# More places for the memory's raw weights and for blocks of x, and an order for down's first operands, in a hybrid decoder block

## The chip, the cores and the metric

One core of a Trainium2 chip runs the whole block in one launch. The time is device microseconds of one execution; the times below are whole executions, the trace is one profiled execution of the kernel, and its rows count from the start of its span.

## The reference

One layer over x (1024 rows of 1024, float32): forgetting attention and stick-breaking attention side by side, cross-attention onto 256 memory rows, and a gated feed-forward part with a short causal convolution. Cut to what matters:

```
h = rmsnorm(x); fq, fk, fv, sq, sk, sv, f_logit = split(h @ w_in)
fox = softmax(fq fk' / 8 + c_t - c_s) fv            # 8 heads of 64, c = cumsum(log_sigmoid(f_logit + b))
sb[t, s] = sigmoid(z) * prod_{s<j<t}(1 - sigmoid(z[t, j]));  sb_o = sb sv     # z = sq sk' / 8
x = x + concat(rmsnorm(fox), rmsnorm(sb_o)) @ w_out
k, v = split(rmsnorm(mem) @ w_mkv)                  # memory: 4 heads of 256
x = x + softmax(rmsnorm(x) w_mq k' / 16) v @ w_mo
u = causal_dwconv(rmsnorm(x) @ w_up, width 3);  gate, val = split(u)
x = x + (silu(gate) * val) @ w_down                 # w_down: 2816 -> 1024
out = rmsnorm(x)
```

## The kernel before

Every product is made of three matmuls of rounded operands: a value is split into a high half (rounded, by ACT or POOL) and a low half (the rest, by DVE), and hi x hi, lo x hi and hi x lo are added up in PSUM (lines 208 to 210). So each weight costs a load into a raw buffer, a high half ("whi") and a low half ("wlo"), each in two parts of 512 columns (lines 402, 407, 412), before PE can use it. The same lines serve all weights of this stage, which are numbered in the order of their use.

**The planned stage.** From line 355 on, the attention with the projections that run beside it is not written in program order: a planner ("Plan") takes operations with an engine, a cost, a due time and counted places, and makes one order for each engine's in-order queue. Score groups pass through "st" (scores, PE), exponentials (ACT), "aw" (a running sum, DVE), a multiply (POOL, line 703), transposes "pt" (PE), their split "pth" (ACT) and "ptl" (DVE), and the product "po" (PE). Between them PE makes projections: at the end of the stage those of the memory ("pk" for keys, "pmv" for values, evacuated to "mk" and "mv"), whose weights are 24 to 39, and then the first mixed products ("pm", the output projection w_out, weights from 40 on). The raw weights stand in a ring of three buffers of 512 columns ("wraw").

**Slots.** Four places of 4096 columns (slots 0 to 3) are used one after another for different things. Slot 3 is free once the last scores of the stick-breaking heads have been read (the key `qkdone["s", 3, 1, 1, "read"]`). It then takes "mxf0", the first half of the mixed rows, written earlier to memory by the stores of the heads' outputs and loaded again by 8 loads (line 865); those are the moving operand of the first pm products.

**Blocks of x.** The output of the first mixed products goes onto x, block by block (8 blocks of 256 rows by 512 columns): a load (line 876), adds by DVE (line 893), a store (line 880). The blocks use a ring of two places, tag "negc". Later the rows of x are loaded again ("xr", line 1025) for the second half of the mixed product. The last row of attention weights has a place of its own, tag "p7", which is free after the last transposes (`chain[0]`).

**Down.** After the up products the down product runs as Strassen-like products over 11 blocks f of the 2816 rows, ordered by the tile framework's own scheduler. Its first product takes the left half of a (the gated values, stored to memory as "a_d") and of w_down: for each f a load of a and of the weight (lines 1847, 1848), then a split of each ("opa", "opb", lines 1537 and 1540). Lines 1856 and 1857 load what later products want of the weights (the right halves and "B22"), line 1920 and POOL's accumulating loads what they want of a. All of them but POOL's are issued by SyncE's queue (SP).

## Time and profile before

| what | us |
|---|---|
| whole executions, median of 3 | 1589.77 (1586.8 to 1596.92) |
| profiled execution | 1587.33 |
| its span | 1585.5 |
| PE busy | 1523.2 |
| DVE busy | 1206.8 |
| ACT busy | 789.8 |
| POOL busy | 534.9 |
| mean granted clock of PE | 0.992 |

The span is what the trace shows, from the first instruction to the last; 1.83 us of the profiled execution lie around it. PE is busy nearly throughout, so a reader looks for the few places where PE is idle or where its matmuls take longer (the granted clock below 1.00), and goes from there to the instruction that released it, and to what that one had waited for.

### The profile page before, as it was taken

To read this page: it belongs to the slowest core of one execution; us is meant where nothing else is said; L and a number is where in the kernel's file an instruction comes from. 1 tells how busy PE (TensorE), PEld (TensorE's weight loads), DVE (VectorE), ACT (ScalarE), POOL (GpSimd) and SP (SyncE) were. 2 spreads that over 40 slices of the span, in tenths; PEclk is the share of its full clock that TensorE was granted. 3 is DMA by queue.
4 is the path that set the end of the run, shared out by engine and by line. 5 is a ranking of instruction groups with operands and counts; after the bars stand their busy time and mean duration, and the time that the engine had idled before them with its cause. 6 is when DMAs were issued, how large, how long until landed. Compare 5 with 4: busy or idle time off the path is not lost.

```text
span 1585.5 us, 22098 instructions
## 1 busy us (share of the span) xinstructions
PE 1523.2 (96%) x7684; PEld 1267.5 (80%) x7684; DVE 1206.8 (76%) x2066; ACT 789.8 (50%) x1558; POOL 534.9 (34%) x656
## 2 busy tenths in 40 slices
PE   7999999999999889999999989999999999999997
PEld 7677888887888767878887767888888888788886
DVE  7377877877877875364548899999999999786575
ACT  7368768767867652043325564333333333445445
POOL 3032323332331310123132256544455442233342
PEclk9999999999999999999999999999999999999999
DMA  5221021011025547412136554222222223998782
GB/s 180 88 74 67 20 69 61 28 67 67 28 67 167 200 146 248 153 50 77 40 107 174 127 164 126 81 93 88 85 80 80 80 82 106 326 293 203 147 185 106
DMA packets 78223, 183.54 MB, mean 116 GB/s; under 512 B 8728, under 2 KB 8856, under 8 KB 77856
## 3 DMA queue, kind: packets, MB, share of 16 engines
q1 hardware_dynamic: 62976, 152.63, 28.1%
q0 software_dynamic: 14688, 29.37, 10.4%
q8 instruction: 60, 0.98, 0.3%
q14 instruction: 51, 0.42, 0.1%
q10 hardware_dynamic: 448, 0.14, 0.0%
HBM read 130.69 MB, written 33.59 MB: 104 GB/s over the span
## 4 chain that ended last, share of the span: by engine, by line
PE 57%; DVE 19%; issue 8%; ACT 7%; DMA 6%; POOL 2%; SPq 0%; POOLq 0%; DVEq 0%; ACTq 0%
PE dn L209 4%; PE dn L210 4%; PE dn L208 4%; PE pt L746 3%; PE up_p L208 3%; PE up_p L209 3%; PE up_p L210 3%; PE pq L208 2%; PE pq L209 2%; PE pq L210 2%; PE po L763 2%; PE pqm L210 2%; DMA wraw<-in_w_dram 2%; PE pqm L209 2%; PE pqm L208 2%
## 5 line engine op out<-in xcount | busy, mean ns | idle before, releaser
L703 POOL TENSOR_TENSOR p<-p,aw 128x383 f32<-128x383 f32 (+4 forms) x64 | 79.6, 1243 | 173.5 <-DVE aw L697 148.9
L750 ACT ACTIVATE pth<-pt 128x512 fp32r<-128x512 f32 x192 | 92.7, 490 | 61.1 <-PE pt L746 55.2
L754 DVE TENSOR_TENSOR ptl<-pt,pth 128x512 fp32r<-128x512 f32 x192 | 103.6, 549 | 25.5 <-ACT pth L750 24.0
L209 PE MATMUL dn<-opb,opa 128*128 128x512 f32 x308 | 120.7, 392 | 2.3 <-DVE opb L1540 2.3
L210 PE MATMUL dn<-opb,opa 128*128 128x512 f32 x308 | 120.6, 391 | 0.0
L208 PE MATMUL dn<-opb,opa 128*128 128x512 f32 x308 | 118.9, 391 | 0.0
L746 PE MATMUL pt<-zid,p 128*128 128x128 f32 x576 | 95.7, 275 | 4.7 <-DVE ptl L754 4.5
L746 PEld LDWEIGHTS pt<-zid,p 128*128 128x128 f32 x576 | 72.6, 142 | 23.9 <-DVE ptl L754 6.9
L1551 POOL TENSOR_TENSOR tmp<-wv 128x512 f32<-128x512 f32 x20 | 33.5, 1674 | 164.1 <-DMA wv<-in_w_dram 158.5
L412 DVE TENSOR_TENSOR wlo<-wraw,whi 128x512 fp32r<-128x512 f32 x84 | 68.0, 838 | 21.5 <-ACT whi L407 21.0
L763 PE MATMUL po<-ptl,v 128*128 128x512 f32 x192 | 68.6, 357 | 9.0 <-DVE ptl L754 8.7
L1779 ACT ACTIVATE yv<-cv,cw 128x1024 f32<-128x1024 f32 x22 | 27.3, 1242 | 99.7 <-DVE cv L1811 98.4
L194 POOL TENSOR_SCALAR whi<-wraw 128x512 fp32r<-128x512 f32 x48 | 30.0, 639 | 134.4 <-issue 44.6
L680 POOL TENSOR_SCALAR p<-p,fx 128x128 f32<-128x128 f32 (+3 forms) x64 | 48.7, 764 | 74.6 <-DVE fx L620 63.9
L209 PEld LDWEIGHTS dn<-opb,opa 128*128 128x128 f32 x308 | 58.1, 189 | 14.6 <-DVE opb L1540 2.7
L208 PE MATMUL up_p<-b,a 128*128 128x512 f32 x176 | 69.3, 394 | 0.0
L762 PE MATMUL po<-pth,v 128*128 128x512 f32 x192 | 68.5, 357 | 0.5 <-ACT pth L750 0.4
L210 PE MATMUL up_p<-b,a 128*128 128x512 f32 x176 | 68.5, 389 | 0.0
L209 PE MATMUL up_p<-b,a 128*128 128x512 f32 x176 | 68.5, 389 | 0.0
L208 PEld LDWEIGHTS dn<-opb,opa 128*128 128x128 f32 x308 | 58.3, 189 | 12.3
L210 PEld LDWEIGHTS dn<-opb,opa 128*128 128x128 f32 x308 | 58.3, 189 | 12.2
L407 ACT ACTIVATE whi<-wraw 128x512 fp32r<-128x512 f32 x84 | 49.9, 626 | 30.6 <-DMA wraw<-in_w_dram 14.8
(513 smaller groups left out, 5227.8 us busy)
## 6 DMA issues: line engine op xcount, KB each, us to landing
wraw<-in_w_dram SPq DMA_DIRECT2D x136, 256.0 KB, 3.0
a_d<-yv SPq DMA_DIRECT2D x22, 512.0 KB, 2.6
wg<-in_w_dram SPq DMA_DIRECT2D x20, 512.0 KB, 3.5
wv<-in_w_dram SPq DMA_DIRECT2D x20, 512.0 KB, 3.5
dn<-a_d POOLq DMA_DIRECT2D x32, 256.0 KB, 7.0
dn<-a_d SPq DMA_DIRECT2D x24, 256.0 KB, 9.2
dn<-in_w_dram SPq DMA_DIRECT2D x24, 256.0 KB, 7.9
xr<-mos POOLq DMA_DIRECT2D x20, 256.0 KB, 6.1
```

Of the source, the lines that this page charges most:

```text
L208: T.matmul(o, lt[0], rt[0], start=start, stop=False)
L209: T.matmul(o, lt[0], rt[1], start=False, stop=False)
L210: T.matmul(o, lt[1], rt[0], start=False, stop=stop)
L407: A.activation(t["hi"][:, c], t["raw", n], AF.Copy)
L412: in_turn("low", lambda: V.tensor_tensor(t["lo"][:, c], t["raw", n], t["hi"][:, c].bitcast(F32), op=ALU.subtract))
L680: G.tensor_scalar(out=c_["p"], in0=c_["p"], scalar1=c_["fx"][:, 4:5], scalar2=0.0, op0=ALU.mult, op1=ALU.add)
L703: G.tensor_tensor(c_["p"][:, :n0 - 1], c_["p"][:, :n0 - 1], c_["a"][:, 1:], op=ALU.mult)
L746: T.transpose(pt[:, j * P:(j + 1) * P], self.rows[j]["p"][:, kb * P:(kb + 1) * P], ident)
L750: A.activation(t[:, 512 - n:], self.sp["pt", kb][:, 512 - n:], AF.Copy)
L754: V.tensor_tensor(t[:, 512 - n:], self.sp["pt", kb][:, 512 - n:], self.sp["th", kb][:, 512 - n:].bitcast(F32), op=ALU.subtract)
L762: T.matmul(self.po[:, c], lv, self.sp["th", kb][:, c], start=kb == 0, stop=False)
L763: T.matmul(self.po[:, c], lv, self.sp["tl", kb][:, c], start=False, stop=kb == 4 * self.g + 3)
```

## The change

- Weights 26 to 37 no longer use the ring of three buffers. Their raw halves go to eight buffers "rx", views of slot 3, which are made when the last stick-breaking scores have been read. The loads of mxf0 into the same slot wait for the last low half that reads rx (`rx_end`). The planner orders the stage anew with these places.
- The sixth and the eighth block of x (those with t2 == 3) use the place of p7, after the last transposes; the others stay in the ring of two.
- In down, the splits of the first product are tied in order (f = 0, 1, 2 ...; each behind the last high half and low half before it). The loads of the second set wait for the issue of the first sixteen loads of the first set, and the loads of a's right halves with POOL's additions for that of the 22 second loads.

```diff
@@ plan
+    RX, rx, rx_end = range(26, 38), [], []
+        raw = "rx" if i in RX else "raw"
             def load(n=n, c=c):
-                t["raw", n] = wp.tile([P, 512], F32, tag="wraw", name=f"wraw{i}", bufs=3)
+                if raw == "rx":
+                    t["raw", n] = rx[(2 * i + n) % 8]
+                else:
+                    t["raw", n] = wp.tile([P, 512], F32, tag="wraw", name=f"wraw{i}", bufs=3)
-            l_ = plan.add(DMA, 900, load, [], ["raw"], at=at, late=1800, behind=b_[0][0])
+            l_ = plan.add(DMA, 900, load, [], [raw], at=at, late=1800, behind=b_[0][0])
-            o_ = plan.add(DVE, dve(512), low, [h_], ["lo"] * (n == 0), ["raw"], at=at, lock=True, behind=b_[0][2])
+            o_ = plan.add(DVE, dve(512), low, [h_], ["lo"] * (n == 0), [raw], at=at, lock=True, behind=b_[0][2])
+            if raw == "rx":
+                rx_end[:] = [o_]
...
-        for th, k, after in ((0, 3, [qkdone["s", 3, 1, 1, "read"]]), (1, 0, line[-1:])):
+        for th, k, after in ((0, 3, rx_end), (1, 0, line[-1:])):
...
+            t = pp.tile([P, D], F32, tag="p7", name="xs") if late_x(nh, t2) else \
+                sw.tile([P, D], F32, tag="negc", name="xs", bufs=2)
...
-                        x_[nh, tb // 2] = plan.add(DMA, 900, lambda nh=nh, tb=tb: load_x(nh, tb // 2), [], ["negc"],
+                        x_[nh, tb // 2] = plan.add(DMA, 900, lambda nh=nh, tb=tb: load_x(nh, tb // 2), chain[0] * late_x(nh, tb // 2),
+                                                   [place(nh, tb // 2)],
...
+            plan.add(DMA, 0, lambda: rx.extend(views(slot(3, "rx", dt=F32).rearrange("p k c -> p (k c)"), 8)), [qkdone["s", 3, 1, 1, "read"]], [], ["rx"] * 8, at=0)
@@ down
-    for f in range(H):
-        nc.sync.dma_start(pb[f][:, hi_], w[dn0 + f, :, hi_])
-        nc.sync.dma_start(B22[f], w[dn0 + H + f, :, hi_])
+    with ExitStack() as behind:
+        for l_ in first_loads[:2 * 8]:
+            behind.enter_context(tc.issue_after(l_.ins))
+        for f in range(H):
+            second_loads += [nc.sync.dma_start(pb[f][:, hi_], w[dn0 + f, :, hi_]),
+                             nc.sync.dma_start(B22[f], w[dn0 + H + f, :, hi_])]
...
-            split_op(oa, fa(f), A)
-            split_op(ob, fb(f), A)
+            for dst, src in ((oa, fa), (ob, fb)):
+                with ExitStack() as behind:
+                    for ins in queue:
+                        behind.enter_context(tc.issue_after(ins))
+                    low = split_op(dst, src(f), A)
+                if in_order:
+                    queue[:] = last_round[0], low
...
-    o = dn_product(lambda f: pa[f][:, lo_], lambda f: pb[f][:, lo_])
+    o = dn_product(lambda f: pa[f][:, lo_], lambda f: pb[f][:, lo_], in_order=True)
...
+    with ExitStack() as behind:
+        for l_ in second_loads[:22]:
+            behind.enter_context(tc.issue_after(l_.ins))
+        for f in range(H):
+            nc.sync.dma_start(pa[f][:, hi_], a_d[f][:, hi_])
+            onto_a(f, hi_, a_d[H + f][:, hi_])
```

The order of the instructions on the engines, at three places. First the memory's projections. SyncE's queue before, from the loads of mxf0 to the first second-half mixed operands:

```order
L865 DMA mxf_6261<-mix_d_3_91 128x512
L865 DMA mxf_6261<-mix_d_3_99 128x512
L402 DMA wraw_6367<-in_w_dram 128x512
L402 DMA wraw_6376<-in_w_dram 128x512
L402 DMA wraw_6391<-in_w_dram 128x512
L402 DMA wraw_6420<-in_w_dram 128x512
L402 DMA wraw_6434<-in_w_dram 128x512
L402 DMA wraw_6449<-in_w_dram 128x512
L402 DMA wraw_6514<-in_w_dram 128x512
L402 DMA wraw_6528<-in_w_dram 128x512
L969 DMA mxs_q_6549<-mix_d_4_92 128x1024
```

And now, the last loads of this stage (the first fourteen rx loads stand where mxf0 stood):

```order
L411 DMA rx<-in_w_dram 128x512 x2
L990 DMA mxs_v_6532<-mix_d_6_102 128x1024
L411 DMA rx<-in_w_dram 128x512 x4
L411 DMA wraw_6829<-in_w_dram 128x512
L411 DMA wraw_6839<-in_w_dram 128x512
L411 DMA wraw_6857<-in_w_dram 128x512
L876 DMA mxf_7022<-mix_d_0_88 128x512
L876 DMA mxf_7022<-mix_d_0_96 128x512
```

The loads of mxf0 have moved from ahead of the memory's weights to behind those of 38 and of 39's first half. DVE's queue in the middle of the stage before (mk is the evacuation of a key product):

```order
L697 SCALAR_TENSOR_TENSOR aw<-st,aw,zid 128x512
L412 TENSOR_TENSOR wlo_6713<-wraw_6615,whi_6693 128x512
L558 TENSOR_TENSOR mk<-pk,mk 128x256
L412 TENSOR_TENSOR wlo_6713<-wraw_6677,whi_6693 128x512
L697 SCALAR_TENSOR_TENSOR aw<-st,zid 128x128
L754 TENSOR_TENSOR ptl<-pt,pth 128x256
L754 TENSOR_TENSOR ptl<-pt,pth 128x128
L412 TENSOR_TENSOR wlo_6756<-wraw_6689,whi_6742 128x512
```

And the same stretch now:

```order
L765 TENSOR_TENSOR ptl<-pt,pth 128x256
L421 TENSOR_TENSOR wlo_6682<-rx,whi_6672 128x512 x2
L569 TENSOR_TENSOR mk<-pk,mk 128x256
L708 SCALAR_TENSOR_TENSOR aw<-st,zid 128x512
L708 SCALAR_TENSOR_TENSOR aw<-st,zid 128x128
L708 SCALAR_TENSOR_TENSOR aw<-st,aw,zid 128x512
L421 TENSOR_TENSOR wlo_6748<-rx,whi_6724 128x512 x2
L569 TENSOR_TENSOR mk<-pk,mk 128x256
L708 SCALAR_TENSOR_TENSOR aw<-st,zid 128x256
L765 TENSOR_TENSOR ptl<-pt,pth 128x128
```

The two halves of a weight stand back to back, and the last split of a group (128x128) has gone from ahead of weight 32's low halves to behind them.

Second the blocks of x, SyncE's queue. Before, from the third load on:

```order
L880 DMA x_d<-xs 128x2x512
L190 DMA wraw_7638<-in_w_dram 128x512
L190 DMA wraw_7644<-in_w_dram 128x512
L876 DMA xs<-in_x_dram 128x2x512
L880 DMA x_d<-xs 128x2x512
L876 DMA xs<-in_x_dram 128x2x512
L1025 DMA xr_7615<-x_d 128x1024
L1025 DMA xr_7616<-x_d 128x1024
L880 DMA x_d<-xs 128x2x512
L876 DMA xs<-in_x_dram 128x2x512
```

And now:

```order
L900 DMA x_d<-xs 128x2x512
L893 DMA xs<-in_x_dram 128x2x512
L190 DMA wraw_7615<-in_w_dram 128x512
L190 DMA wraw_7621<-in_w_dram 128x512
L893 DMA xs<-in_x_dram 128x2x512
L900 DMA x_d<-xs 128x2x512
L893 DMA xs<-in_x_dram 128x2x512
L900 DMA x_d<-xs 128x2x512
```

A load now stands ahead of the store that it followed, and no reload of x stands between the blocks: all eight come behind the last store.

Third down's first loads, SyncE's queue. Before:

```order
L1847 DMA dn_13082<-a_d_65 128x512
L1848 DMA dn_13082<-in_w_dram 128x512
L1847 DMA dn_13082<-a_d_66 128x512
L1848 DMA dn_13082<-in_w_dram 128x512
L1856 DMA dn_13082<-in_w_dram 128x512 x2
L1920 DMA dn_13082<-a_d_65 128x512
L1920 DMA dn_13082<-a_d_66 128x512
L1847 DMA dn_13083<-a_d_67 128x512
L1848 DMA dn_13083<-in_w_dram 128x512
```

And now, from the same load on:

```order
L1867 DMA dn_13059<-a_d_65 128x512
L1868 DMA dn_13059<-in_w_dram 128x512
L1867 DMA dn_13059<-a_d_66 128x512
L1868 DMA dn_13059<-in_w_dram 128x512
L1867 DMA dn_13060<-a_d_67 128x512
L1868 DMA dn_13060<-in_w_dram 128x512
L1867 DMA dn_13060<-a_d_68 128x512
L1868 DMA dn_13060<-in_w_dram 128x512
L1867 DMA dn_13061<-a_d_69 128x512
```

The loads of the second set (L1856, L1920) have left the place between f = 1 and f = 2; they stand behind f = 7 now.

## Rows read from the trace of the kernel before

**Rows 1.** The page: busy time of each engine with its share of the span and its instructions, and the shares of the chain that ended last by engine.

```profile
PE 1523.2 (96%) x7684; PEld 1267.5 (80%) x7684; DVE 1206.8 (76%) x2066; ACT 789.8 (50%) x1558; POOL 534.9 (34%) x656
...
PE 57%; DVE 19%; issue 8%; ACT 7%; DMA 6%; POOL 2%; SPq 0%; POOLq 0%; DVEq 0%; ACTq 0%
```

**Rows 2.** The busy time of each engine in stretches of the span (from:to, length, then busy us and instructions of PE, its weight loads, DVE, ACT and POOL, the granted clock of PE, the busy share of the DMA engines, and GB/s).

```profile
500.00:590.00 90.00, 78.44 (x473) 68.34 (x472) 74.12 (x108) 61.29 (x131) 23.74 (x34) 0.96 0.54 176
520.00:530.00 10.00, 9.15 (x71) 8.64 (x70) 9.41 (x15) 8.08 (x16) 3.78 (x4) 1.00 0.69 248
560.00:570.00 10.00, 7.81 (x41) 6.34 (x40) 8.19 (x13) 8.19 (x18) 1.68 (x3) 0.98 0.38 109
570.00:580.00 10.00, 10.00 (x43) 8.10 (x42) 7.16 (x11) 5.87 (x12) 3.07 (x4) 0.85 0.25 67
580.00:590.00 10.00, 7.10 (x27) 5.41 (x26) 9.87 (x12) 5.73 (x10) 2.33 (x2) 0.83 0.57 185
630.00:640.00 10.00, 8.41 (x29) 6.48 (x30) 4.04 (x6) 0.00 (x0) 0.62 (x1) 0.83 0.90 323
1370.00:1380.00 10.00, 7.71 (x32) 5.96 (x31) 8.63 (x13) 5.52 (x7) 1.75 (x2) 0.93 1.08 339
1380.00:1390.00 10.00, 10.00 (x41) 8.22 (x40) 10.00 (x16) 6.25 (x12) 2.57 (x3) 0.90 1.08 333
```

**Rows 3.** The timeline of PE: start in us of the span, us, line, operation, and in brackets the idle time before it and what released it.

```profile
539.09 0.39 PE L763 MATMUL po<-ptl,v 128*128 128x256 f32 x1 [2.00 <-DVE ptl L754]
...
547.58 0.66 PE L746 MATMUL pt<-zid,p 128*128 128x128 f32 x4 [1.55 <-DVE ptl L754]
...
568.19 0.45 PE L644 MATMUL st<-k1s,qs 128*128 128x384 f32 x1 [2.19 <-DVE aw L697]
...
569.91 0.63 PE L209 MATMUL pmv<-wlo,mT 128*128 128x512 f32 x1
...
586.94 0.80 PE L208 MATMUL pm<-whi,mxf 128*128 128x512 f32 x1 [2.48 <-DVE mv L558]
...
630.83 0.56 PE L208 MATMUL pm<-whi,mxf 128*128 128x512 f32 x1 [2.32 <-DVE xs L893]
...
638.91 0.50 PE L208 MATMUL pm<-whi,mxf 128*128 128x512 f32 x1 [0.75 <-DVE xs L893]
...
1362.93 0.39 PE L208 MATMUL dn<-opb,opa 128*128 128x512 f32 x1
1363.16 0.39 PE L209 MATMUL dn<-opb,opa 128*128 128x512 f32 x1
...
1377.17 0.50 PE L209 MATMUL dn<-opb,opa 128*128 128x512 f32 x1 [2.29 <-DVE opb L1540]
```

**Rows 4.** The page's costliest groups, one form of down's matmuls: busy us, mean ns of one, idle us just before them and what ended most of it.

```profile
L209 PE MATMUL dn<-opb,opa 128*128 128x512 f32 x308 | 120.7, 392 | 2.3 <-DVE opb L1540 2.3
```

**Rows 5.** The timeline of ACT, the high halves of the memory's weights that waited for a transfer.

```profile
536.78 0.63 ACT L407 ACTIVATE whi<-wraw 128x512 fp32r<-128x512 f32 x1 [2.90 <-DMA wraw<-in_w_dram]
...
539.66 0.63 ACT L407 ACTIVATE whi<-wraw 128x512 fp32r<-128x512 f32 x1 [1.25 <-DMA wraw<-in_w_dram]
...
565.58 0.63 ACT L407 ACTIVATE whi<-wraw 128x512 fp32r<-128x512 f32 x1 [0.85 <-DMA wraw<-in_w_dram]
...
578.60 0.63 ACT L407 ACTIVATE whi<-wraw 128x512 fp32r<-128x512 f32 x1 [0.55 <-DMA wraw<-in_w_dram]
```

**Rows 6.** The timeline of SyncE's queue (SPq): when a run of loads began to be issued, for how long, and how many they are.

```profile
501.57 3.72 SPq L865 DMA_DIRECT2D mxf<-mix_d  x8
505.39 17.42 SPq L402 DMA_DIRECT2D wraw<-in_w_dram  x8
...
538.41 47.39 SPq L402 DMA_DIRECT2D wraw<-in_w_dram  x19
```

**Rows 7.** The timeline of DVE, adds of the first mixed products onto x that waited for the block of x.

```profile
629.93 1.41 DVE L893 SCALAR_TENSOR_TENSOR xs<-pm,rsg,xs 128x512 f32<-128x512 f32 x2 [1.70 <-DMA xs<-in_x_dram]
...
638.10 1.41 DVE L893 SCALAR_TENSOR_TENSOR xs<-pm,rsg,xs 128x512 f32<-128x512 f32 x2 [2.45 <-DMA xs<-in_x_dram]
643.79 1.64 DVE L893 SCALAR_TENSOR_TENSOR xs<-pm,rsg,xs 128x512 f32<-128x512 f32 x2 [4.28 <-DMA xs<-in_x_dram]
```

**Rows 8.** SyncE's queue again: a store of an x block and the load of the next.

```profile
625.71 0.39 SPq L880 DMA_DIRECT2D x_d<-xs  x1
...
632.47 0.38 SPq L876 DMA_DIRECT2D xs<-in_x_dram  x1
```

**Rows 9.** The chain that ended last, the transfer ahead of down's late operands: start us, us, what.

```profile
1357.45 11.34 DMA dnq<-a_d
```

**Rows 10.** The timeline of ACT at the start of down.

```profile
1365.52 0.63 ACT L1537 ACTIVATE opa<-dn 128x512 fp32r<-128x512 f32 x1 [8.45 <-DMA dn<-a_d]
```

**Rows 11.** The timeline of DVE, two pairs of low halves (weights 40 and 41).

```profile
582.38 3.07 DVE L412 TENSOR_TENSOR wlo<-wraw,whi 128x512 fp32r<-128x512 f32 x2
...
587.62 1.29 DVE L412 TENSOR_TENSOR wlo<-wraw,whi 128x512 fp32r<-128x512 f32 x2
```

**Rows 12.** The timeline of POOL, the last row's multiply.

```profile
582.61 2.29 POOL L703 TENSOR_TENSOR p<-p,aw 128x1023 f32<-128x1023 f32 x1 [7.91 <-DVE aw L697]
```

**Rows 13.** The transfers issued from 500 to 660: how many, KB each, median us from issue to landing.

```profile
mxf<-mix_d SPq DMA_DIRECT2D x16, 256.0 KB, 5.2
...
xr<-x_d SPq DMA_DIRECT2D x8, 512.0 KB, 5.5
```

More of the change, by code (lines that the diff above doesn't have):

```diff
@@ L267, in hybrid_block, with views @@
     vp = ctx.enter_context(tc.tile_pool(name="vp", bufs=3, reuse_waits="tile"))
+    def views(t, n):
+        return [t[:, i * 512:(i + 1) * 512] for i in range(n)]
     def slot_list(k, nm, kc=KC):
@@ L355, in hybrid_block @@
     plan = Plan({"P": 2, "S": 3, "T": 2, "O": 1, "th": NT, "tl": NL, "aw": 2, "ost": 2, "fx": 4, "raw": 3, "nm": 2,
-                 "hi": 0, "lo": 0, "negc": 2, "v": 3} | {f"p{i}": 1 for i in range(TB)})
+                 "hi": 0, "lo": 0, "rx": 0, "negc": 2, "v": 3} | {f"p{i}": 1 for i in range(TB)})
     PE, ACT, DVE, POOL, DMA = "PE", "ACT", "DVE", "POOL", "DMA"
@@ L871, in mixed_first, with late_x, place @@
                                           [r_] + stored["f"][th::2], at=0, late=2600) for a in range(2)]
+        def late_x(nh, t2):
+            return t2 == 3
         def load_x(nh, t2):
             rows = slice(t2 * 2 * P, (t2 + 1) * 2 * P)
-            xs[nh, t2] = sw.tile([P, D], F32, tag="negc", name="xs", bufs=2).rearrange("p (b c) -> p b c", b=2)
+            t = pp.tile([P, D], F32, tag="p7", name="xs") if late_x(nh, t2) else \
+                sw.tile([P, D], F32, tag="negc", name="xs", bufs=2)
+            xs[nh, t2] = t.rearrange("p (b c) -> p b c", b=2)
             nc.sync.dma_start(xs[nh, t2], x[rows, nh * 512:(nh + 1) * 512].rearrange("(b p) c -> p b c", p=P))
+        def place(nh, t2):
+            return "p7" if late_x(nh, t2) else "negc"
         def store_x(nh, t2):
@@ L921, in mixed_first @@
                         z_ = plan.add(DMA, 100, lambda nh=nh, tb=tb: store_x(nh, tb // 2), [e_], at=at, late=2000)
-                        plan.add(DMA, 0, lambda: None, [z_], [], ["negc"], at=at)
+                        plan.add(DMA, 0, lambda: None, [z_], [], [place(nh, tb // 2)], at=at)
     def load_negc(h, at):
@@ L1390, in hybrid_block @@
     ti = to + 8
-    def views(t, n):
-        return [t[:, i * 512:(i + 1) * 512] for i in range(n)]
     def retile(k, nm, dt=F32):
@@ L1539, in split_op @@
             G.tensor_scalar(out=dst[0], in0=src, scalar1=1.0, scalar2=0.0, op0=ALU.mult, op1=ALU.add)
-        V.tensor_tensor(dst[1], src, dst[0].bitcast(F32), op=sub)
+        return V.tensor_tensor(dst[1], src, dst[0].bitcast(F32), op=sub).ins
     def prep_gate(n):
@@ L1845, in hybrid_block @@
     dn0 = ti
+    first_loads, second_loads = [], []
     for f in range(H):
-        nc.sync.dma_start(pa[f][:, lo_], a_d[f][:, lo_])
-        nc.sync.dma_start(pb[f][:, lo_], w[dn0 + f, :, lo_])
+        first_loads += [nc.sync.dma_start(pa[f][:, lo_], a_d[f][:, lo_]),
+                        nc.sync.dma_start(pb[f][:, lo_], w[dn0 + f, :, lo_])]
     vq = [vp.tile([P, 2, 1024], F32, tag="v", name=f"dnv{i}") for i in range(3)]
@@ L1877, in hybrid_block @@
     step = 0
+    queue = []
     def op_tile(nm):
@@ L1883, in op_tile, with dn_product @@
         return pairs(pool.tile([P, 1024], F32R, tag=tag, name=f"op{nm}"))
-    def dn_product(fa, fb, held=0, done=None, ready=None):
+    def dn_product(fa, fb, held=0, done=None, ready=None, in_order=False):
         nonlocal step
@@ L1913, in dn_product @@
         return o
-    o = dn_product(lambda f: pa[f][:, lo_], lambda f: pb[f][:, lo_])
+    o = dn_product(lambda f: pa[f][:, lo_], lambda f: pb[f][:, lo_], in_order=True)
     for f in range(H):
         onto_a(f, lo_, a_d[f][:, hi_])
-    for f in range(H):
-        nc.sync.dma_start(pa[f][:, hi_], a_d[f][:, hi_])
-        onto_a(f, hi_, a_d[H + f][:, hi_])
+    with ExitStack() as behind:
[4 more added lines that the diff above has]
+            onto_a(f, hi_, a_d[H + f][:, hi_])
     for j in range(4):
```

## The prediction, before the result was known

> **What bounds the kernel now.** I read the page's busy shares and its chain first, then the windows of the two places that the change touches, then each idle row there. TensorE (PE) is busy 96% of the span [rows 1], so the only time to be had is what it stands idle or runs at the lower clock. The chain runs through VectorE (DVE) for 19% and through transfers for 6% [rows 1]: these few stretches are what the change can reach. Three of them matter.
>
> The first is the stretch of the memory's projections, 500 to 590 us. PE is busy 78.44 of 90 us there, so 11.56 are idle, and the granted clock falls to 0.85 and 0.83 in its last two windows [rows 2]. The long gaps behind 530 are 2.00, 1.55, 2.19 and 2.48 us [rows 3]; at 569.91 a matmul of 512 columns takes 0.63 us [rows 3], where the mean of the same shape is 0.39 [rows 4]: the lower of the two levels (1.2 of 2.4 GHz). Such a stretch follows the 2.19 gap and another follows the 2.48 gap. Where PE waits for DVE's "ptl" or "aw", DVE is late because its in-order queue holds a weight's low half before them, that low half waits for ScalarE's (ACT's) high half, and ACT waits for the raw weight's transfer: 2.90, 1.25, 0.85 and 0.55 us at 536.78, 539.66, 565.58 and 578.60 [rows 5]. The transfers are late because they are issued late: 8 loads spread over 17.42 us and 19 over 47.39 us [rows 6], each one waiting until a low half has freed one of three buffers.
>
> The second is the end of the first mixed products: PE waits 2.32 and 0.75 us at 630.83 and 638.91 [rows 3] for DVE's adds onto x, and those wait for the x block itself, 1.70, 2.45 and 4.28 us [rows 7]. A block's load stands in the queue next to the store that frees its place: the store is issued at 625.71, the load that uses that place at 632.47 [rows 8]. The window 630 to 640 has a clock of 0.83 [rows 2].
>
> The third is the start of down: one gap of 2.29 us at 1377.17 [rows 3], the only idle time of all 308 matmuls of its form [rows 4], and a clock of 0.93 and 0.90 in the two windows around it [rows 2]. The chain there is a transfer of 11.34 us [rows 9], and ACT stood 8.45 us for one of them [rows 10].
>
> **The raw weights of the memory.** No instruction of an engine is added or taken away: the same 24 half loads, 24 high and 24 low halves, in another order. With eight buffers, the loads of 26 to 37 go out as soon as the slot is free. A buffer comes free four weights earlier than its next use instead of one and a half, so ACT's four waits of 5.6 us altogether [rows 5] should go. What they cost PE: the gaps 2.00, 1.55 and 2.19, since the ptl and aw behind the late low halves come in time; and the half-clock stretch after the last, (0.02 + 0.15) x 10 = 1.7 us in the windows 560 to 580 [rows 2]. Together 7.4 us. What is idle ahead of 530 stays, as the loads there are the old ones. The 2.48 at 586.94 stays with its half-clock stretch ((1 - 0.83) x 10 = 1.7): the products wait there for the last "mv" evacuation, behind a pair of low halves that took 3.07 us instead of the 1.29 of the same pair five us later [rows 11], because GpSimd (POOL) multiplied the widest row, 2.29 us, at that time [rows 12]. That pair and that multiply still stand side by side in the new order.
>
> Against the gain stands that DVE has little air: 74.12 of 90 us, and 9.41 of 10 in 520 to 530 [rows 2]. The new order puts the two halves of a weight back to back, sixteen times; a pair that meets a POOL multiply holds DVE 3.07 - 1.29 = 1.8 us longer, with the next ptl behind it, which in the old order often stood between the halves. I charge 1.0 us: one such pair more on PE's path than before, less what slack a PE queue with projections ahead of the ptl's user gives. So 7.4 - 1.0 = **6.4 us**. Bounds: below, nothing gained and one pair's 1.8 us lost; above, the 7.4 plus half of the 2.48 gap and its half-clock stretch, (2.48 + 1.7) / 2 = 2.1, so 9.5.
>
> The Trainium skill speaks against pairing here. Its page "SBUF — State Buffer", section "Who interferes with whom", says that a VectorE instruction with two SBUF inputs and a GpSimd one that reads SBUF share a read interface, and that the later of them is held until the first is through. By that rule a pair met by the 2.29 us multiply would take up to 1.29 + 2.29 = 3.58 us, and the charge would be 2.3 and not 1.8 a meeting; the trace, with 3.07, lies under it.
>
> The slot has a price. It held the first operand of the first mixed products, "mxf0", whose 8 loads went out at 501.57 [rows 6], 85 us before use. They now wait for the last low half of weight 37, at about 563 by the old rows moved up by the first half's gain; 8 loads took 3.72 us to issue [rows 6] and 5.2 us each to land [rows 13], so the operand is whole at about 572. The products begin at 586.94 - 6.4 = 580.5. I cost it at nothing, with 8 us of cover. One raw load (39's second half) now stands behind these 8 on SyncE's queue and may be a microsecond late; that lies within the charge.
>
> **Two x blocks in the last row's place.** The sixth block's load needs no store any more, only the last transposes, so it goes out ahead of the third's store; its adds, and the gaps 2.32 and 0.75, move off the path, with the half-clock stretch after the first, (1 - 0.83) x 10 = 1.7 us. That is **4.8 us**. The eighth block waits for the sixth's store as before, but the next products no longer wait for its adds: what uses x after them is the reload of all rows, which in the new order stands whole behind the last store. In my walk of the queue the last store goes out at 643 (on the old clock) and the first reload, with 5.5 us to land [rows 13], is there at about 649, one or two us before the first add that needs it. I cost that at nothing. Bounds: 1.5 us, if the reload is 3.3 us late (one block's 4.28 wait less that 1 us of air); 4.8 at the top.
>
> **Down in order.** The first operands' loads now go strictly f = 0, 1, 2 ... with no half of the second set between them, and ACT and DVE prepare in that order. Before, six halves that later products want (four weights, two rows of a) stood among the first sixteen loads, and the operand issued at 1357.45 took 11.34 us [rows 9]. Without them sixteen loads of 256 KB, at the 333 GB/s of the window 1380 to 1390 [rows 2] 0.8 us each, from 1342 on are in by about 1358 with a landing time behind the last. That is f up to 7. PE starts at 1362.93 and a matmul follows another by 0.23 us [rows 3], so with 12 to an f it needs f = 4 at 1374 and f = 8 at 1385. So the 2.29 gap goes, and with it the half-clock stretch of (0.07 + 0.10) x 10 = 1.7 us [rows 2]: **4.0 us**. The 22 second loads and POOL's additions start later; they are needed by the second and third products, 30 us of PE each, so I cost their delay at nothing. The cover is gone if they come 10 us late. Bounds: 0, if another operand is late instead; 4.0. The in-order tie also puts DVE and ACT work of the last up rows behind operands that wait; the nearest row is ACT's 8.45 us [rows 10], which cost PE only 2.29 then, so I set the lower bound at -2.
>
> The Trainium skill has a rule on this, too. "DMA: Bandwidth & Descriptors", section "Issuing engines are not separate DMA queues", says that transfers run on the same 16 engines whoever starts them. By it POOL's additions share with the wanted loads, and holding them back is worth what they took; the same bytes still have to pass, and a later product might pay. No row of down after 1390 shows idle time, so there is room.
>
> **The sum.** 6.4 + 4.8 + 4.0 = 15.2 us. The profiled execution took 1587.33 us, 1.83 of it around its span of 1585.5, and is 2.4 below the median of 1589.77. From it the sum gives 1572.1; from the median, which the times are compared with, **1574.6**.
>
> **Rivals.** *DVE is the bound (20%).* For: the full windows and the pairs above; a new wait of po or pt for ptl behind pairs would replace the old. Against: DVE stands idle 15.9 of those 90 us [rows 2], which the earlier raw weights make usable. The first part then returns 2 us: 1589.77 - 2 - 4.8 - 4.0 = 1579. *Gains handed on (15%).* The x rows' reload or a late down operand takes back its part: 6.4 + 1.5 + 0 gives 1582, both with the first rival's 2 us 1586. *All of it and more (15%).* Nothing new is late, the pair beside the multiply moves off the mv: 9.5 + 4.8 + 4.0 gives 1571.5, and if the smaller gaps of the first stretch go as well, some 3 us more, 1568. *Slower than before (6%).* One mechanism: mxf0's loads. They wait in order on the queue for the last low half of 37; if that comes after about 571 instead of 563, every us more is a us of PE. It is slower than before from 15 us more, at 586, about when the old kernel's DVE was through with weight 40's first pair [rows 11]; three us beyond that it gives 1592. Against it: nothing else stands between the low half and the loads on the queue.
>
> My forecast keeps 44%. **Chances** (about 1% is what a measurement of this kernel can tell from no change): faster by over 1% means below 1573.9; half of the forecast's share less a little (0.20) and the 0.15 of "all and more" with some of the rest make 0.38. Slower by over 1%, above 1605.7, 0.03. The rest, 0.59, within 1%. The range holds all but the slow rival, the far end of "handed on" and the far end of "more": 1567 to 1585.
>
> **What would show it.** Right: ACT's high halves wait for no raw transfer between 515 and 575; no PE gap over 1.3 us in 520 to 575 and a granted clock of 1.00 there; the first mixed product some 6 us earlier against the score groups; no wait of pm for xs, clock 1.00 in the window where it was 0.83; no gap in dn and 1.00 around it. Wrong: PE waiting for ptl after a low pair of 2 to 3 us; pm waiting for mxf; the reload's add waiting for xr by over a us; a gap between dn products 2 and 3.

## The result, and the profile after

The changed kernel takes 1577.21 us (median of 6 runs, 1574.85 to 1582.41) against 1589.92 us of the kernel before, run beside it. The ratio is 0.9915, with a 95% interval from 0.9899 to 0.9932: faster by 0.85%, which is 13.5 us (the two medians themselves lie 12.7 us apart). The profiled execution has a span of 1573.1 us, 12.4 less than before.

The page of the changed kernel, with its busy times, the chain's shares and one form of down's matmuls, answers [rows 1, 4]:

```profile
PE 1519.0 (97%) x7684; PEld 1265.6 (80%) x7684; DVE 1207.3 (77%) x2066; ACT 788.9 (50%) x1558; POOL 532.0 (34%) x656
...
PE 76%; DVE 9%; issue 6%; ACT 6%; DMA 2%; POOL 1%; SPq 0%; POOLq 0%; DVEq 0%; ACTq 0%
...
L209 PE MATMUL dn<-opb,opa 128*128 128x512 f32 x308 | 119.8, 389 | 0.0
```

PE is busy 4.2 us less than before and the span is 12.4 us shorter: 8 of the 12 us were idle time, and the rest matmuls at the lower clock. In the chain, transfers went from 6% to 2% and DVE from 19% to 9%. The idle time of down's matmuls is gone.

The windows (same columns as [rows 2]) show where:

```profile
500.00:590.00 90.00, 83.18 (x507) 72.60 (x506) 78.16 (x113) 63.19 (x133) 23.78 (x34) 0.98 0.60 200
580.00:590.00 10.00, 8.91 (x39) 7.33 (x40) 7.03 (x12) 4.55 (x8) 0.32 (x2) 0.83 0.75 241
630.00:640.00 10.00, 10.00 (x45) 8.28 (x45) 2.33 (x4) 0.00 (x0) 0.00 (x0) 1.00 0.59 194
1370.00:1380.00 10.00, 10.00 (x46) 8.29 (x45) 8.38 (x15) 5.30 (x11) 2.23 (x3) 1.00 1.10 298
```

PE has 83.18 busy of 90 us instead of 78.44. The granted clock is 1.00 where it was 0.83 (630 to 640) and 0.93 (1370 to 1380); it is still 0.83 from 580 to 590. To compare stages whose start has shifted, I measure from the first start of one kind of matmul to the first (or last) of another:

| stage (first or last start of a PE form) | before | after |
|---|---|---|
| start of the span to first key product | 502.0 | 503.5 |
| first key product to first mixed product | 85.0 | 78.5 |
| first to last mixed product | 103.1 | 99.3 |
| last mixed product to first of the memory's queries | 1.8 | 1.8 |
| from there to the first up product | 236.2 | 236.9 |
| first up product to first down product | 434.9 | 435.1 |
| first to last down product | 213.4 | 209.2 |
| from there to the end of the span | 9.1 | 8.7 |

The three stages that the change touches give 6.5, 3.8 and 4.2 us. What stands against them, 1.6 us ahead of the first key product and 0.8 us later, lies in stages that the change does not touch. Over the fourteen traces of this document the first of these ranges from 501.6 to 504.8 us and the other from 235.9 to 240.5, so such differences come from one execution to the next.

The idle rows of PE in the first and second of these stages, timeline as in [rows 3]:

```profile
542.90 0.33 PE L774 MATMUL po<-ptl,v 128*128 128x128 f32 x1 [2.64 <-DVE ptl L765]
...
581.09 0.33 PE L774 MATMUL po<-ptl,v 128*128 128x128 f32 x1 [1.99 <-DVE ptl L765]
...
582.00 0.39 PE L208 MATMUL pm<-whi,mxf 128*128 128x512 f32 x1
...
582.59 0.63 PE L210 MATMUL pm<-whi,mxf 128*128 128x512 f32 x1
...
624.72 0.47 PE L208 MATMUL pm<-whi,mxf 128*128 128x512 f32 x1 [0.53 <-DVE xs L913]
```

The gaps of 2.00, 1.55, 2.19 and 2.48 us of [rows 3] are gone, also the last, which was forecast to stay. Two new ones of 2.64 and 1.99 us have come, both a "po" that waits for the last split of its group, and half-clock matmuls (0.63 us) follow the second. The first mixed product starts without a wait.

### The profile page after: what moved, and what is told of

The parts are those of the page before. It is cut to its first block, busy times and chain, and to the rows that moved or that the text cites. A ratio compares the mean times of both kernels' runs of the same rounds, so it can differ in the third digit from the quotient of the medians.

```text
span 1573.1 us, 22084 instructions
## 1 busy us (share of the span) xinstructions
PE 1519.0 (97%) x7684; PEld 1265.6 (80%) x7684; DVE 1207.3 (77%) x2066; ACT 788.9 (50%) x1558; POOL 532.0 (34%) x656
## 4 chain that ended last, share of the span: by engine, by line
PE 76%; DVE 9%; issue 6%; ACT 6%; DMA 2%; POOL 1%; SPq 0%; POOLq 0%; DVEq 0%; ACTq 0%
PE up_p L208 8%; PE up_p L210 8%; PE up_p L209 8%; PE dn L208 4%; PE dn L210 4%; PE dn L209 4%; PE pt L757 3%; PE pq L208 2%; PE pq L209 2%; PE pq L210 2%; PE po L774 2%; PE pqm L210 2%; PE pqm L209 2%; PE pqm L208 2%; PE po L773 2%
## 5 line engine op out<-in xcount | busy, mean ns | idle before, releaser
L209 PE MATMUL dn<-opb,opa 128*128 128x512 f32 x308 | 119.8, 389 | 0.0
L210 PE MATMUL dn<-opb,opa 128*128 128x512 f32 x308 | 119.8, 389 | 0.0
L774 PE MATMUL po<-ptl,v 128*128 128x512 f32 x192 | 68.8, 358 | 10.4 <-DVE ptl L765 10.3
L708 DVE TENSOR_TENSOR_SCAN aw<-st,zid 128x128 f32<-128x128 f32 (+1 forms) x64 | 51.8, 816 | 16.1 <-ACT st L702 15.5
L1836 ACT ACTIVATE yg<-yg 128x1024 f32<-128x1024 f32 x22 | 23.3, 1061 | 77.3 <-DVE yg L1801 77.3
```

The source lines that it names most:

```text
L209: T.matmul(o, lt[0], rt[1], start=False, stop=False)
L210: T.matmul(o, lt[1], rt[0], start=False, stop=stop)
L708: V.tensor_tensor_scan(out=a[:, c0:e][:, ::-1], data0=c_["st", n][:, :w_][:, ::-1], data1=zid[:, 512 - w_:][:, ::-1] if diag else zid[:, : ...
L774: T.matmul(self.po[:, c], lv, self.sp["tl", kb][:, c], start=False, stop=kb == 4 * self.g + 3)
```

## The experiments

### Each part alone

The three parts were put in by themselves. The first with only the buffers:

```diff
         def late_x(nh, t2):

-            return t2 == 3
+            return False
...
-    o = dn_product(lambda f: pa[f][:, lo_], lambda f: pb[f][:, lo_], in_order=True)
+    o = dn_product(lambda f: pa[f][:, lo_], lambda f: pb[f][:, lo_])
-        for l_ in first_loads[:2 * 8]:
+        for l_ in []:
-        for l_ in second_loads[:22]:
+        for l_ in []:
```

> Only the eight buffers for the memory's weights (with the planner's order that they give and mxf0's later loads); x blocks and down as before. Theory: the stage from the first key product to the first mixed product is its own, so this part returns its 6.4 us whatever the others do: from 85.0 us in the trace of before to about 78.5, ACT's high halves wait for no transfer there, and the time is about 0.996 of before. The wait for x (2.32) and the gap in down (2.29) stay. Rival: the x part needs the earlier start and this part the x part (blocks of x move in the same order), then the x waits grow and the time falls by 3 us or less (0.998). Of the four long gaps of before, those of 2.00, 1.55 and 2.19 are gone, and two new ones stand behind the pairs that meet the widest multiply, 2.6 and 2.0 us.

Measured: 0.9959 (0.9947 to 0.9971). First key to first mixed product: 79.9 us; the two new gaps are there with the same 2.64 and 1.99 us; the waits for x are 2.03 and 1.75 us, so the x part is not helped or hurt by this one. PE's idle time in the stage (without a gap of 1.2 us near its start that every trace has) is 5.58 us, the same as in the whole change; the 1.4 us more of the stage go with a half-clock stretch in it, of which the change's trace has none there. So the part returns its idle time by itself, as the theory had it.

The x blocks alone (the rx buffers, their wait and down's edits taken out):

```diff
-    RX, rx, rx_end = range(26, 38), [], []
+    RX, rx, rx_end = range(0), [], []
-        for th, k, after in ((0, 3, rx_end), (1, 0, line[-1:])):
+        for th, k, after in ((0, 3, [qkdone["s", 3, 1, 1, "read"]]), (1, 0, line[-1:])):
```

> Only the two x blocks in the last row's place. Theory: the mixed products, first to last, take 56.9 us before and about 53 here, as in the whole change; the time is about 0.997 of before. The half-clock stretch at 630 goes with the gap of 2.32. Rival: without the earlier start of the first part the p7 place comes free too late for the sixth block's load and the gap stays; then no difference (1.000).

Measured: 0.9957 (0.9943 to 0.9971). First to last mixed product: 99.0 us, one wait for x of 0.54 us left. The p7 place is free early enough without the first part.

Down alone (the edits of the two diffs above that take out the buffers and the x blocks):

> Only down's order and held loads. Theory: no idle time of PE between down's products, granted clock 1.00 there; from down's first to last product 213.0 us before, about 209 here; the time 0.997 of before. Rival: a second gap opens where the held loads are wanted (second or third product), and the time is within 1 us of before.

Measured: 0.9969 (0.9952 to 0.9985). First to last down product: 209.2 us, no wait of PE in it. No later gap.

The three ratios multiply to 0.9885, the whole change has 0.9915. The intervals (about 0.0025 either way on the product) overlap, the difference of 0.0030 is as large as its own uncertainty, and no stage of the whole change's trace is more than 0.3 us longer than in the part alone; whether the parts take a little from each other stays open.

### How many buffers

> The whole change, but with four rx buffers in place of eight. Theory: the gain of the first part is the lead of the loads; with four buffers a load waits for the low half two weights before it instead of four, ACT waits for transfers again (2 to 5 us in all between 500 and 590) and the first mixed product comes 2 to 5 us later than with eight, ratio to before 0.993 to 0.995. Rival: the gain is the planner's new order with any buffers beyond the ring of three, then four do as well as eight (0.9915) and ACT waits for no transfer.

```diff
-                    t["raw", n] = rx[(2 * i + n) % 8]
+                    t["raw", n] = rx[(2 * i + n) % 4]
...
-            plan.add(DMA, 0, lambda: rx.extend(views(slot(3, "rx", dt=F32).rearrange("p k c -> p (k c)"), 8)), [qkdone["s", 3, 1, 1, "read"]], [], ["rx"] * 8, at=0)
+            plan.add(DMA, 0, lambda: rx.extend(views(slot(3, "rx", dt=F32).rearrange("p k c -> p (k c)"), 8)), [qkdone["s", 3, 1, 1, "read"]], [], ["rx"] * 4, at=0)
```

Measured: 0.992 (0.9893 to 0.9948), the first stage 79.9 us long. ACT's one wait of size for these weights, on its timeline:

```profile
540.56 1.24 ACT L416 ACTIVATE whi<-rx 128x512 fp32r<-128x512 f32 x2 [1.37 <-DMA rx<-in_w_dram]
```

It is 1.37 us, and PE's idle time in the stage (without the gap near its start) is 5.58 us, as with eight. The rival was right on the time and on PE: four do as well, though ACT still waits a little. (This trace is of the slowest of the four executions, 1583.28 us; the others took 1576.33 to 1578.4.) So I tried three, the depth of the old ring, in the same way.

> The whole change, but with three rx buffers, as deep as the old ring. Theory now (four did as well as eight): what helped is not the depth but what stands ahead of the loads and the order around them; mxf0's 2 MB no longer stand at the head of the queue, and the planner puts the halves in pairs. Then three do nearly as well as eight too: from the first key product to the first mixed product idle of PE is 5 to 7 us (10.3 before, 5.6 with eight) and the ratio to before is 0.991 to 0.993. Rival: depth does decide, between three and four; then ACT waits 4 to 6 us for transfers as before, the idle time is back at 9 to 10 us, and the ratio is 0.995 to 0.996.

Measured: 0.993 (0.9908 to 0.9952). ACT's timeline and PE's:

```profile
540.87 0.63 ACT L416 ACTIVATE whi<-rx 128x512 fp32r<-128x512 f32 x1 [3.64 <-DMA rx<-in_w_dram]
```

```profile
543.39 0.47 PE L774 MATMUL po<-ptl,v 128*128 128x128 f32 x1 [3.85 <-DVE ptl L765]
```

ACT waits 5.6 us in all, as much as before [rows 5], now 3.64 of it at once, and PE stands 3.85 us behind it. So ACT's waits for transfers hang on the depth, between three and four. For PE the answer lies between theory and rival: its idle time in the stage is 7.7 us, against 10.3 before the change (10.1 to 11.0 in the five traces with the old code there) and 5.6 with four or eight. About half of the saving thus comes with three buffers already. What it is owed to (mxf0's loads behind the weights, the planner's new order, or a second ring beside the old one) was not separated.

The stage takes 85.0 us, as before the change, but 5.1 us of it went to half-clock stretches in this execution, against 1.8 in the trace of before. In time, three buffers cannot be told from four or eight: the interval holds 0.992 and 0.9915. (The rival's ratio of 0.995 to 0.996 had left out the other two parts, which alone multiply to 0.9926.)

### The two new gaps

DVE's timeline and POOL's at both places in the changed kernel:

```profile
538.67 3.06 DVE L421 TENSOR_TENSOR wlo<-rx,whi 128x512 fp32r<-128x512 f32 x2
...
542.59 0.26 DVE L765 TENSOR_TENSOR ptl<-pt,pth 128x128 fp32r<-128x128 f32 x1
...
577.76 3.07 DVE L421 TENSOR_TENSOR wlo<-wraw,whi 128x512 fp32r<-128x512 f32 x2
580.76 0.28 DVE L765 TENSOR_TENSOR ptl<-pt,pth 128x128 fp32r<-128x128 f32 x1
```

```profile
538.83 2.36 POOL L714 TENSOR_TENSOR p<-p,aw 128x1023 f32<-128x1023 f32 x1 [0.73 <-DVE aw L708]
...
577.99 2.29 POOL L714 TENSOR_TENSOR p<-p,aw 128x1023 f32<-128x1023 f32 x1 [3.92 <-DVE aw L708]
```

A pair of low halves takes 3.06 and 3.07 us while the multiply of 1023 columns runs, and the split of 128 columns that PE wants comes behind the pair. It is the collision of [rows 11, 12], which before held up the evacuation. Three repairs were tried on the whole change. The first puts the split ahead:

```diff
-                l_ = [plan.add(DVE, dve(n), lambda kb=kb, n=n: self.low(kb, n), h_ + l_, ["tl"], ["T"], at=at)]
+                l_ = [plan.add(DVE, dve(n), lambda kb=kb, n=n: self.low(kb, n), h_ + l_, ["tl"], ["T"], at=at - 0.8 * (pr == 3 and kind == "s" and kb == nkb - 1))]
```

> The whole change, with one more edit: the planner takes the last split of a group of the last stick-breaking heads (128 columns) ahead of a weight's low halves when both are ready. Theory: the two new waits of PE (2.64 and 1.99 us) are the price of a pair of low halves that meets POOL's widest multiply with that split behind it; with the split ahead of the pair both waits go, though the pair still takes 3 us, and with the second goes the half-clock stretch after it: 4.6 to 6.3 us, ratio to before 0.988, below the change's 0.9915. Rival: the pair delays what else PE waits for (the key products' weights, the values' evacuation), so that the wait moves to the next product and 2 us or less are won.

Measured: 0.9932 (0.9914 to 0.9949), not better than the change. PE's timeline:

```profile
542.43 1.05 PE L831 MATMUL pss<-cst,sqaccf 128*128 128x1 f32 x8 [2.74 <-DVE ost L786]
...
586.19 0.79 PE L208 MATMUL pm<-whi,mxf 128*128 128x512 f32 x1 [3.73 <-DVE mv L569]
```

and DVE's:

```profile
536.70 0.26 DVE L765 TENSOR_TENSOR ptl<-pt,pth 128x128 fp32r<-128x128 f32 x1
...
538.07 3.07 DVE L421 TENSOR_TENSOR wlo<-rx,whi 128x512 fp32r<-128x512 f32 x2
...
541.72 0.66 DVE L786 TENSOR_TENSOR ost<-po,ost 64x512 f32<-64x512 f32 x1
...
581.62 3.07 DVE L421 TENSOR_TENSOR wlo<-wraw,whi 128x512 fp32r<-128x512 f32 x2
...
585.44 0.69 DVE L569 TENSOR_TENSOR mv<-pmv,mv 128x512 fp32r<-128x512 f32 x1
```

The split is ahead of the pair now (536.70), the pair still takes 3.07 us, and what stands behind it is late instead: "ost", for which a row-sum product waits 2.74 us, and the evacuation "mv", for which the first mixed product waits 3.73 us. The rival was right: the wait moved on.

The second keeps the low halves away from the multiply:

```diff
                     slow = s.lock and other and locked[other] > now
+                    if slow and getattr(s, "apart", False):
+                        continue
...
+            o_.apart = i in range(26, 42)
```

> The whole change, with one more edit: in the planner a low half of weights 26 to 41 does not begin while POOL's multiply runs. Theory: the loss is the 1.8 us that the pair and the widest multiply cost DVE when they meet, twice in this stage; kept apart, a pair takes 1.3 us everywhere, both waits of 2.6 and 2.0 us fall below 1 us and no wait takes their place: 3 us or more, ratio to before 0.989 or below. Rival: DVE has no air, so a wait of the same size moves to what stands behind (the values' evacuation or the first mixed products), and the ratio is 0.991 or above.

Measured: 0.9921 (0.9904 to 0.9938). Low halves from rx, grouped (busy us and mean ns of one), in the changed kernel and here:

```profile
L421 DVE TENSOR_TENSOR wlo<-rx,whi 128x512 fp32r<-128x512 f32 x24 | 21.0, 915 | 1.3 <-ACT whi L416 1.2
```

```profile
L423 DVE TENSOR_TENSOR wlo<-rx,whi 128x512 fp32r<-128x512 f32 x24 | 16.3, 711 | 4.4 <-ACT whi L418 4.4
```

The halves fell from 915 to 711 ns each, and behind 520 no wait of PE in the stage is over 0.9 us; the granted clock is 1.00 in every window from 500 to 650. (One of the 24 still meets a multiply.) Yet from the first key to the last mixed product it takes 177.6 us, against 177.8: thirteen short waits of 0.2 to 0.9 us, 6.1 us in all, stand in the place of the long ones and the small ones beside them, 7.2 us in all. The theory was right on the collision and wrong on the gain: over this stretch DVE works 112.2 us instead of 119.8, and PE gains nothing by it. PE itself is busy 0.8 us longer, though it has no half-clock stretch here; why is open. The first matmul behind most of the short waits takes some 0.1 us more than its mean, which is a part of it.

The third gives the widest multiply of these heads to DVE, with and without the edit of the split:

```diff
-                    o_ = plan.add(POOL, 200 + n0 * 2.3, lambda i=i, c_=c_: self.sb4(i, c_), [s_] + pos, [], ["aw"], at=at,
-                                  lock=True)
+                    on_v = i == 7 and pr == 3
+                    o_ = plan.add(DVE if on_v else POOL, dve(n0) if on_v else 200 + n0 * 2.3,
+                                  lambda i=i, c_=c_, e=V if on_v else G: self.sb4(i, c_, e), [s_] + pos, [], ["aw"], at=at,
+                                  lock=not on_v)
```

> The edit of rx_ptl (the last split of a group ahead of the low halves), and the widest multiply of the last stick-breaking heads made by DVE and not by POOL. DVE gets two multiplies of about 1.2 us and loses two collisions of 1.8 us. Theory: the waits that moved in rx_ptl (2.74 and 3.73 us) came from the held pair, so they shrink by 0.6 us each and by what the multiply's end comes earlier (2.3 us on POOL, 1.2 on DVE): 4 us of idle time in the stage and a ratio of 0.990 or below. Rival: DVE's own work is what PE waits for, then adding to it changes nothing (0.993).

Measured: 0.9917 (0.9903 to 0.9932). The idle time of PE in the stage is 4.5 us, about what the theory said, but the ratio did not follow it.

> The whole change, and the widest multiply of the last stick-breaking heads made by DVE and not by POOL, without the edit of the split. Theory: the pair ahead of the split takes 1.3 us instead of 3.06, and the multiply (1.2 us) stands ahead of the split too: the 2.64 us wait falls to about 2, the 1.99 one to below 1; idle time from the first key product to the first mixed product 4 to 5 us where the change has 5.6. Rival: the wait moves, idle time 6 us or more.

Measured in one execution: 1573.83 us. The idle time in the stage, 4.9 us, is what the theory said, but not the waits that it is made of: at the first place, where about 2 us were expected, they are 0.57 and 0.40, at the second, where less than 1 was, 2.16. From the first key to the last mixed product it takes 176.5 us, 1.3 less than the change. That is less than single executions of one kernel differ by, so it is not shown to be faster. None of the repairs clearly beats the change.

### What mxf0's wait would cost

> The whole change, but the eight buffers serve weights 26 to 39, so that mxf0's loads wait for the last low half of 39, some 12 us later than with 37. This prices the rival in which mxf0 comes too late. Theory: the low half ends at about 576 on the clock of the change, the eight loads need 8 to 10 us, the first mixed product starts at 585 or later instead of 582, after a wait for mxf of 3 to 5 us that stands in the trace as a wait for a transfer. Rival: what PE waits for is still the split and the values' evacuation, and the loads are hidden; then the first mixed product comes within 1 us of the change's.

```diff
-    RX, rx, rx_end = range(26, 38), [], []
+    RX, rx, rx_end = range(26, 40), [], []
```

Measured in one execution: 1585.08 us, 3.6 of it outside its span. SyncE's queue and PE:

```profile
575.09 3.66 SPq L876 DMA_DIRECT2D mxf<-mix_d  x8
...
579.59 6.94 SPq L876 DMA_DIRECT2D mxf<-mix_d  x8
...
587.55 1.62 SPq L411 DMA_DIRECT2D wraw<-in_w_dram  x3
```

```profile
582.05 0.80 PE L208 MATMUL pm<-whi,mxf 128*128 128x512 f32 x1 [2.49 <-DVE mv L569]
...
598.50 0.50 PE L208 MATMUL pm<-whi,mxf 128*128 128x512 f32 x1 [4.41 <-ACT whi L416]
```

mxf0's loads go out at 575.09, ten us later than the 564.71 of the change, and the first mixed product still starts at 582.05, for mv and not for mxf0. So ten us more are still hidden from the products that read mxf0: the rival of this run was right. The prediction's slower rival counted every us behind 571 against PE; here the last low half of rx ends at 575.1, and no product waits for mxf0. The time is lost behind it: the planner has put the next weights' high halves on ACT behind the splits and evacuations of the last group, and PE waits 4.41 us for one of them at 598.50; first to last mixed product takes 107.0 instead of 99.3 us. The raw weights behind mxf0's second half come late on the queue as well (587.55), but on ACT's timeline from 578 to 600 no high half waits for a transfer; so in this execution it is the order of ACT's queue that costs. Whether the late loads are why the planner chose that order was not separated.

### Down: the order and the held loads

Both without the buffers and the x blocks; the first without the two waits of loads, the second without the order:

```diff
-        for l_ in first_loads[:2 * 8]:
+        for l_ in []:
...
-        for l_ in second_loads[:22]:
+        for l_ in []:
```

> Of the change only the tie of down's first operands in order; the loads are not held. Theory: the loads' order is what the gap hangs on, so the 2.29 us gap stays or grows to 3 to 5 us, because the operands now wait in order for the late transfers. Rival: the preparing order alone closes the gap; then no idle time in down.

PE's timeline, and ACT's wait for the last store of a:

```profile
1379.91 0.49 PE L208 MATMUL dn<-opb,opa 128*128 128x512 f32 x1 [1.07 <-ACT opb L1555]
1381.39 0.50 PE L209 MATMUL dn<-opb,opa 128*128 128x512 f32 x1 [0.99 <-DVE opb L1558]
```

```profile
1377.58 1.24 ACT L1797 ACTIVATE yv<-cv,cw 128x1024 f32<-128x1024 f32 x1 [8.59 <-DMA a_d<-yv]
```

```diff
-    o = dn_product(lambda f: pa[f][:, lo_], lambda f: pb[f][:, lo_], in_order=True)
+    o = dn_product(lambda f: pa[f][:, lo_], lambda f: pb[f][:, lo_])
```

> Of the change only the held loads of down; the operands are not tied. Theory: with the first sixteen loads ahead of the others the gap goes (0 to 0.5 us of idle time in down), and first to last product takes 209 us, as in the whole change. Rival: the scheduler prepares out of order as before, and a gap of 1 us or more stays.

PE's timeline:

```profile
1379.53 0.50 PE L209 MATMUL dn<-opb,opa 128*128 128x512 f32 x1 [1.70 <-DVE opb L1558]
```

Neither closes the gap by itself, by one trace of each: 1.07 and 0.99 us are left with the order, 1.70 with the held loads, 2.29 with neither [rows 3], none with both. First to last down product takes 213.5 us (1.7 of it by a half-clock stretch) and 211.3, against 209.2 with both. My theory that the held loads suffice is wrong, and so is the rival that the order does. With the order alone, ACT waits 8.59 us for the slot of gated rows whose store stands on the queue behind loads of the second set.

## Why the prediction was right, and where it was not

**The sum.** 15.2 us were forecast, 13.5 came (10.8 to 16.1 by the interval); 1577.21 lies in the range and the change is within 1%, to which 0.59 was given. The three terms can be measured better than in one pair of traces, since some of the experiments leave a stage as it was in before, and others as it is in after. (Runs whose edits go beyond the three parts are left out.)

| term | forecast | stage with the old code | with the new code | measured |
|---|---|---|---|---|
| memory's weights | 6.4 | 85.0, 85.6, 86.2, 86.4, 86.5 | 78.5, 79.9 | 6.8 |
| x blocks | 4.8 | 102.0, 102.2, 103.1, 104.0, 104.9 | 99.0, 99.3 | 4.1 |
| down | 4.0 | 211.7, 213.2, 213.4 | 209.2 | 3.6 |

The measured terms add up to 14.5 us, by the means of each row.

**The memory's weights: the right sum by a wrong working.** The waits of ACT went and the gaps of 2.00, 1.55 and 2.19 with them, as forecast. The gap of 2.48 was to stay and went. The charge of 1.0 us for "one such pair more on PE's path" was too small: the two pairs cost PE 2.64 and 1.99 us. So PE's idle time in the stage (without the 1.23 at its start, which all traces have) fell from 10.33 to 5.58 us, 4.75, where the steps (5.74 of gaps less 1.0) gave 4.74: a charge too small by 3.6 met gaps that went beyond those counted (2.48 and the small ones). The step that failed is "That pair and that multiply still stand side by side", from which I let the mv wait stay: they do, but what stands behind them is another instruction. The rest of the term, 1.7 us, is one half-clock stretch less, which is partly luck (below): the change's trace has none in this stage, that of its first part alone has one. The reason given, a lead of four weights, was too much as well: a lead of two does the same, and with the old depth about half of the idle time went already.

The rival that DVE is the bound (20%) named the waits that came, "a new wait of po or pt for ptl behind pairs", which the prediction also listed as a sign of being wrong; the rival was wrong on what they would leave of the term, 2 us. In its favour, three ways of removing these two waits brought 0.9917, 0.9921 and 0.9932, against 0.9915, so the stage gave no more. But it is not the amount of DVE's work that holds PE: with 7.5 us less of it nothing was won.

The Trainium skill's rule in "SBUF — State Buffer", "Who interferes with whom", is borne out in kind: kept apart from the multiply, a low half takes 711 ns in the mean. For a pair that meets it the prediction's bound by the rule was 3.58 us; the traces have 3.06 and 3.07. In these two, and in the pair of [rows 11], the first half began 0.16 to 0.23 us before the multiply, and the pair ended 0.54 or 0.55 us behind the multiply's end (541.73 and 541.19, 580.83 and 580.28). So one half of the pair was held and not both, which is why the pair stays under the bound.

**mxf0.** The last low half of 37 was to be done at about 563; the loads were issued at 564.71:

```profile
503.16 17.91 SPq L411 DMA_DIRECT2D rx<-in_w_dram  x14
...
564.71 3.66 SPq L876 DMA_DIRECT2D mxf<-mix_d  x8
```

The product began at 582.00 without a wait. The cover was enough, and with the loads ten us later it still was; what cost time there was the order of the weights behind mxf0.

**The x blocks: right mechanism, 0.7 us too much.** The sixth block's load goes out ahead of a store, and the reloads of x behind the last:

```profile
604.96 0.38 SPq L893 DMA_DIRECT2D xs<-in_x_dram  x1
608.78 0.38 SPq L900 DMA_DIRECT2D x_d<-xs  x1
...
631.26 5.81 SPq L900 DMA_DIRECT2D x_d<-xs  x2
637.12 4.80 SPq L1047 DMA_DIRECT2D xr<-x_d  x8
```

Eight reloads are issued from 637.12; the first add that needs one, at 643.64, waits for POOL and not for a load, so the air of "one or two us" was there. What is left is 0.53 us, and DVE's timeline says why:

```profile
622.21 1.69 DVE L197 TENSOR_TENSOR wlo<-wraw,whi 128x512 fp32r<-128x512 f32 x2 [2.68 <-POOL whi L194]
623.83 1.40 DVE L913 SCALAR_TENSOR_TENSOR xs<-pm,rsg,xs 128x512 f32<-128x512 f32 x2
```

The block is there, but the adds stand behind two low halves of POOL's weights. The term had counted every wait for x as a wait for its transfer. It had also counted the half-clock stretch as certain; it came in four of the five traces with the old code, and in the fifth waits of 2.35 and 2.23 us for x had none behind them.

**Down: right, less the certainty of the half-clock stretch.** The gap is gone in every run that has both edits, and no later product waits, so the delayed second loads are covered as forecast. The 1.7 us for the clock were counted as always there; in one of three executions with the old code (211.7 us) the gap, 2.14 us there, had no such stretch after it. That the order ties DVE and ACT to late operands, bounded at -2, cost PE nothing: in the changed kernel ACT waits 3.26 us for the store of a, and no product of down waits; with the order alone it waits 8.59 us, and PE 2.06.

**The rivals handed on and slower** did not occur. "All of it and more" needed the pair off the path, and the pair stayed on it.

## What to carry to other kernels

When a ring of buffers is deepened, look first for the depth at which the idle time of the bounding engine stops falling (here at four halves; three brought about half of the saving), and not for the largest that fits. When a low-priority pair of instructions moves in an in-order queue, ask what will stand behind it at its new place, and whether it still meets the other engine that slows it down. And count how often a cost occurs over several executions before it is put into a sum as certain.

## What the runs showed of the hardware

**The clock's fall is a matter of the execution.** The same code has the same gap, and the clock falls after it in one execution and not in another. PE's timeline and the window around it, in the kernel with the x blocks alone:

```profile
542.04 0.39 PE L774 MATMUL po<-ptl,v 128*128 128x256 f32 x1 [2.02 <-DVE ptl L765]
```

```profile
540.00:550.00 10.00, 7.98 (x52) 7.77 (x52) 6.98 (x12) 5.96 (x15) 2.93 (x7) 0.83 0.51 175
```

and in the one with down's held loads alone, whose engines execute the same instructions in the same order up to there:

```profile
540.97 0.39 PE L774 MATMUL po<-ptl,v 128*128 128x256 f32 x1 [2.02 <-DVE ptl L765]
```

```profile
540.00:550.00 10.00, 7.49 (x57) 6.88 (x58) 8.58 (x17) 6.19 (x14) 3.41 (x7) 1.00 0.56 177
```

A gap of 2.02 us is followed by a window at 0.83 in the one and at 1.00 in the other; in the kernel before, with the same order again, the gap of 2.00 us had 1.00 in that window. Over the fourteen traces, the loss of granted clock from 500 to 650 us (the missing share of the clock times the length) came in multiples of 1.7 us: none to four of them, three in before, one in after, and one to four in the four experiments whose first stage has the old code. In the trace with no wait over 0.9 us behind 520 there was none. So a gap of 2 us costs itself, and 1.7 us more in some executions; a sum from one trace carries an error of a few times 1.7 us by that alone.
